# Long-convolution and recurrence block on one core: one position sum per tile, and the filter network issued ahead of the first chunk

## The chip, the core and the metric

The kernel runs on one core of a Trainium2 chip. A core has five engines with queues of their own, which run in order: PE (matmul), DVE (vector), ACT (scalar), POOL (GpSimd) and SP, which here only issues transfers. ACT issues transfers too. The metric is the device time of one execution in microseconds (us); lower is better.

## The reference

4096 tokens of 1024 columns get a position table added (512 columns by grid row, 512 by grid column), are normalised and modulated, and go through one input projection. One half of its columns feeds a long convolution with a filter that a small network makes from the position, the other half a gated recurrence in both directions that starts from the states of 256 context tokens. What matters here:

```python
xl = x + grid_sincos(rows, D)[None]                     # the position sum, 4096 x 1024
pl = (rms_norm(xl, norm_g) * (1.0 + sc_l) + sh_l) @ w_in
pc = (rms_norm(ctx, norm_g) * (1.0 + sc_c) + sh_c) @ w_in
...
h = sin(freq[0] * (z @ f_w1 + f_b1))                    # the filter network, 4096 positions x 64
h = sin(freq[1] * (h @ f_w2 + f_b2))
h = sin(freq[2] * (h @ f_w3 + f_b3))
h = h @ f_w4 * exp(-t * deltas)                         # the filter rows
...
hf_c, hb_c = rglru_bidir(pc[..., r0:r1], *rnn_p, zero, zero)
hf_l, hb_l = rglru_bidir(pl[..., r0:r1], *rnn_p, hf_c[:, -1], hb_c[:, 0])
...
y = concat(rms_norm(long_conv(v * x1, k) * x0) * silu(z_h), rms_norm(hf_l + hb_l) * silu(z_r))
out = rms_norm(xl + g_l * (y @ w_out), final_g)
```

`f_w1` to `f_w3` are 64 columns wide; two halves of the positions share a 128-row tile.

## The kernel before

**Start.** `pass_a` first computes the modulation: `mod` (L319) loads `w_mod` in pieces (tile `wm`, 4 buffers) and multiplies them with the condition, part 1 for the scale `s1`, part 0 for the shift. Beside it the first 512 tokens are loaded as two pairs of tiles (`xload`, L402), and the four blocks of `xr` weights.

**A pair of token tiles.** `xload` loads two tiles of 128 tokens (`xt`, 128x1024) by SP and the row part of the positions (`rp`, L413) by the ACT queue. Its inner function `sums` then adds, on POOL, `rp` to columns 0 to 511 and `self.cpos` to columns 512 to 1023 (L421 and L422; both go through the helper line L463), `squares` takes sums of squares on ACT (L432). `xsplit` (L442) scales on DVE (L454), splits the product into two 16-bit parts (`xh` by ACT, L456; `xlo` by POOL, L458) and transposes both by DMA into the chunk tile `X` (L459, L460). Tokens come to `X` by these transposes alone, and `X` of a chunk must be whole before its first matmul.

**Chunks.** Eight chunks of 512 tokens follow. Each has 12 weight blocks (4 `xr`, then 4 pairs `x1`, `v`); a block is 24 matmuls of 128x512 (`inproj`) and a short convolution on ACT and DVE (`conv`, L529 to L542). One block is one step: `tick` (L571) runs what `at` has put on that step. In chunk 0 the weights are still being prepared (`wprep`, L484, L489), and the context tokens go through the same weights (`ctx_in`, matmuls named `R` and `I`).

**The filter.** `mlp` (L830) is the network as a generator with ten stops: for each half of the positions three layers, each on two tiles of 512 columns, then two stops that split the result and write it to `hD`. One tile of one layer is two f32 matmuls (`fb<-x` or `fa<-x`), ACT's `Identity` (L849), five DVE operations (L850 to L854) and ACT's `Sin` (L855); a result is split by L861, L862 and L864 and written by ACT-issued transfers (L868 to L875). Before, its ten stops are pulled at steps 1 to 10 (`ML`, `MK`). `filt` at step `FS` = 10 sets up the filter's constants (`filter_setup`, loads L881 to L898), and 16 groups of 4 filter rows follow from step `FS + FG`, one group every `FD` = 4.95 steps (`filter_group`, `filter_row`). A row takes 3 f16 matmuls (`fa<-whl,hb`), 2 f32 matmuls (`fb<-kd,st`) and two passes each on ACT and DVE, and POOL adds it to `acc`.

**Order.** Within the bounds of the steps a scheduler sets the order of every engine; each queue then runs in that order on the chip. After the eight chunks the Fourier transforms, the backward recurrence and the output follow, which the change does not touch.

Of the kernel before, what the change touches and what calls it, by code (L numbers as in the profile page):

```python
# [10 lines left out]
F32 = mybir.dt.float32  # L11
# [11 lines left out]
D = 1024  # L23
# [6 lines left out]
CT = 5  # L30
ML = 1
MK = 1
FS = 10
RQ = 1
OD = 7
OP1 = (0, 0)
# [11 lines left out]
MS = ()  # L48
XS = ((1, 1, 2), (1, 2, 3))
PB = {"mm": 3, "fa": 2, "fb": 2, "sm": 1}  # L50
FD = 4.95
XK = ((6, 9), (0, 4))
NX = 11
D0 = (8, 11, 12, 13, 14, 16, 17, 17)
# [109 lines left out]
class K:  # L164
# [237 lines left out]
    def xload(self, pool, src, pos, xts=None, rp=None, lag=None):  # L402


        nc = self.nc
        xts = xts or [pool.tile([128, D], F32, name="xt", bufs=2) for k in range(2)]
        ss = pool.tile([128, 2], F32, name="ss", bufs=2)
        if pos is not None:
            q = nc.scalar if rp is not None or RQ else nc.sync
            rp = pool.tile([128, 2, 512], F32, name="rp", bufs=1) if rp is None else rp  # L410
            t = self.a["t_pos"]
            for h in range(2):
                q.dma_start(rp[64 * h:64 * h + 64], bass.AP(  # L413
                    tensor=t.tensor, offset=t.offset + 512 * (2 * pos + h), ap=[[0, 64], [1024, 2], [1, 512]]))
        for k in range(2):
            xt = xts[k]
            nc.sync.dma_start(xt, src[128 * k:128 * k + 128])

        def sums():
            for k, xt in enumerate(xts):  # L420
                self.padd(xt[:, :512], xt[:, :512], rp[:, k])  # L421
                self.padd(xt[:, 512:], xt[:, 512:], self.cpos)  # L422
                if pos > 3:
                    nc.sync.dma_start(self.xpD[128 * (pos + k):128 * (pos + k) + 128], xt)

        def squares():
            with ExitStack() as es:
                if lag and IA[0]:
                    es.enter_context(self.tc.issue_after(self.eva))
                for k in range(2):  # L430
                    xh = pool.tile([128, D], F16, name="xh", bufs=2)
                    nc.scalar.activation(xh, xts[k], AF.Square, accum_out=ss[:, k:k + 1])  # L432
        if lag:
            self.at(lag[0], sums)
            self.at(lag[1], squares)
        else:
            if pos is not None:
                sums()
            squares()
        return xts, ss  # L440
# [144 lines left out]
    def pass_a(self):  # L585
        tc, nc, a = self.tc, self.nc, self.a
        with ExitStack() as es, ExitStack() as right:
            ap = es.enter_context(tc.tile_pool(name="ap", bufs=1))
# [8 lines left out]
            ml = ml_.__enter__()  # L597
            sp_ = tc.tile_pool(name="start", bufs=1)
            sp = sp_.__enter__()
            if True:  # L600
                self.columns(sp)
                self.tap_sums()
                m = self.mod(sp, ml, ap, 1)
                next(m)
                self.cpos = ap.tile([128, 512], F32, name="cpos")
                for h in range(2):
                    nc.scalar.dma_start(self.cpos[64 * h:64 * h + 64], a["t_pos"])
                xt = [hy.tile([128, 1028], F32, name="xc", bufs=4)[:, :D] for k in range(3)]
                xr = [self.xload(ap, tok(0), 0, xt[:2], xt[2].rearrange("p (k c) -> p k c", k=2)),
                      self.xload(ap, tok(2), 2)]  # L610
                raw = self.xp_.tile([128, NB, 8, 128], F32, name="X", bufs=2)
                for j in range(NB):
                    nc.sync.dma_start(raw[:, j], a["w_in"][COLS["xr"] + j])
                self.pull(m)
                m = self.mod(sp, ml, ap, 0)
                next(m)
                for k in range(2):
                    self.xsplit(ap, xr[k], self.s1, self.sx, dst(X, 2 * k))
                gs = [self.wprep("xr", j, raw[:, j]) for j in range(NB)]
                for k in range(2):  # L620
                    for j, g in enumerate(gs):
                        W["xr", j] = next(g)
                self.pull(m)
                for g in gs:
                    next(g)

            def wpair(k):
                raw = sp.tile([128, 2, 8, 128], F32, name="wm", bufs=4)
# [13 lines left out]
            def filt():  # L642
# [4 lines left out]
                next(g)  # L647
                for d in FL:
                    self.at(d, lambda: next(g))
            mlp = self.mlp(ml)  # L650
            for k in range(4):
                self.at(k, lambda k=k: wpair(NB + 2 * k))
            self.at(3, recur)
# [2 lines left out]
            ctx = self.ctx_in(ap, hy, W)  # L656
            for d in (0, 2, 4):
                self.at(CT + d, lambda: next(ctx))
            for k in range(10):
                self.at(ML + k // MK, lambda: self.pull(mlp, 1))  # L660
            self.at(FS, filt)
            for n in range(16):
                self.at(FS + FG + int(FD * n), lambda n=n: self.filter_group(self.flt, n))
# [163 lines left out]
        return zip(*[self.unit(rn, [(0, 2 * p), (0, 2 * p + 1)], n, xcs[p], fin((2 * p, 2 * p + 1))) for p in range(2)])  # L827


    def mlp(self, pool):  # L830
        nc, a = self.nc, self.a
        ws = pool.tile([128, D], F32, name="bm", bufs=1)[:, :384].rearrange("p (l c) -> p l c", l=3)
        nc.scalar.dma_start(ws, a["f_w"])
        fc = pool.tile([128, 6], F32, name="fc")
        nc.vector.tensor_mul(fc[:, 0:3], self.col[:, 104:107], self.col[:, 107:110])
        nc.vector.tensor_copy(fc[:, 3:6], self.col[:, 107:110])
        for half in range(2):
            H = []
            for c in (2 * half, 2 * half + 1):
                z = pool.tile([66, 512], F32, name="x", bufs=4)  # L840
                nc.scalar.dma_start(z, a["t_z"][:, 512 * c:512 * c + 512])
                H.append(z)
            for l in range(3):
                for c in range(2):
                    ps = self.pst("fa" if c % 2 else "fb", 2)
                    self.mms(ps, ws[:66 if l == 0 else 128, l, :], H[c], True, True)
                    x = pool.tile([128, 512], F32, name="x", bufs=4)
                    q = pool.tile([128, 512], F32, name="q", bufs=3)
                    nc.scalar.activation(x, ps, AF.Identity, bias=fc[:, l:l + 1], scale=fc[:, 3 + l:4 + l])  # L849
                    nc.vector.tensor_scalar(q, x, INV2PI, MAGIC, op0=OP.mult, op1=OP.add)  # L850
                    nc.vector.tensor_scalar(q, q, -MAGIC, None, op0=OP.add)
                    nc.vector.scalar_tensor_tensor(x, q, -C1, x, op0=OP.mult, op1=OP.add)
                    nc.vector.scalar_tensor_tensor(x, q, -C2, x, op0=OP.mult, op1=OP.add)
                    nc.vector.tensor_scalar(x, x, PI_IN, -PI_IN, op0=OP.min, op1=OP.max)  # L854
                    nc.scalar.activation(x, x, AF.Sin)  # L855
                    H[c] = x
                yield
            for c in (2 * half, 2 * half + 1):
                h = H[c % 2]
                hl = pool.tile([128, 2, 512], F16, name="q", bufs=3)  # L860
                nc.scalar.activation(hl[:, 0], h, AF.Copy)  # L861
                nc.vector.tensor_sub(hl[:, 1], h, hl[:, 0])  # L862
                hr = pool.tile([128, 2, 512], F16, name="q", bufs=3)
                nc.vector.tensor_copy(hr, hl[:, :, ::-1])  # L864
                lv = hl.rearrange("p x (n m) -> p x n m", m=64)
                rv = hr.rearrange("p x (n m) -> p x n m", m=64)
                n0 = 8 * c
                nc.scalar.dma_start(self.hD[0:64, :, n0:n0 + 8, :], lv[0:64])  # L868
                nc.scalar.dma_start(self.hD[0:64, :, 32 + n0:40 + n0, :], lv[64:128])
                nc.scalar.dma_start(self.hD[64:128, :, 25 - n0:33 - n0, :], rv[64:128])  # L870
                k = 7 if c == 0 else 8
                nc.scalar.dma_start(self.hD[64:128, :, 57 - n0:57 - n0 + k, :], rv[0:64, :, 0:k, :])
                if c == 0:
                    nc.scalar.dma_start(self.hD[64:128, :, 0, 1:64], rv[0:64, :, 7, 0:63])
                    nc.scalar.dma_start(self.hD[64:128, :, 0, 0:1], rv[0:64, :, 7, 63:64])  # L875
                yield
# [85 lines left out]
    def filter_l1(self, pool, kd):  # L962

        nc = self.nc
        ps = self.pst("sm", 1)
        for b in range(NB):
            self.mm(ps[:, b:b + 1], self.acc[:, 128 * b:128 * b + 128], self.ones[:, 0:1], True, True)
        self.rl = self.cp.tile([128, NB], F32, name="rl")
        nc.vector.tensor_copy(self.rl, ps[:, :NB])
        nc.vector.reciprocal(self.rl, self.rl)  # L970
        ps = self.pst("sm", 1)
        self.mm(ps[0:1, :], self.ones[:, 0:1], self.acc, True, True)
        br = pool.tile([1, 512], F32, name="br", bufs=1)
        nc.scalar.dma_start(br, self.a["hy_bias"])
        nc.vector.tensor_mul(br, ps[0:1, :], br)
        nc.vector.tensor_add(kd[0:1, :], kd[0:1, :], br)
# [544 lines left out]
```

## Time and profile before

| | |
|---|---|
| median of 3 runs | 2239.83 us (2232.47 to 2243.20) |
| the profiled execution, its own time | 2242.97 us |
| its span from the first to the last instruction | 2241.2 us |
| mean granted clock of TensorE over the span | 0.943 of full speed |
| PE, DVE, ACT, POOL busy | 86%, 61%, 52%, 28% of the span |

The profile is of one execution. A span lies 1.8 us inside that execution's time. A row of the timeline says when an instruction started, how long it took, and in brackets how long its engine had been idle before it and what ended that. A row of a group says how often it ran, its busy time and the mean of one; matmul rows overlap a little, so sums of such rows are upper bounds of the engine's busy time. Granted clock 1.00 is 2.4 GHz; below that, part of a stretch ran at 1.2 GHz.

### The profile page before, as it was taken

How to read it: one execution, taken by the hardware profiler on the slowest of the kernel's cores; microseconds unless marked ns; L12 is line 12 of the kernel's file. 1: busy time of each engine (PE TensorE's matmuls, PEld its weight loads, DVE VectorE, ACT ScalarE, POOL GpSimd, SP SyncE). 2: the span in 40 equal slices, each digit the busy share in tenths (PEclk: the TensorE clock that was granted, in tenths of full speed). 3: DMA queues.
4: the chain of work that ended last, by engine and by line, in shares of the span. 5: the costliest groups of instructions: out<-in, count | busy, mean ns of one | idle time of the engine just before them, and what ended most of it. 6: DMA issues, size and time to landing. Idle time of an engine off the chain costs nothing. (4 is left out here: it accounts for less than half of the span.)

```text
span 2241.2 us, 30015 instructions
## 1 busy us (share of the span) xinstructions
PE 1934.0 (86%) x10640; PEld 933.0 (42%) x10640; DVE 1362.1 (61%) x2629; ACT 1173.0 (52%) x1828; POOL 623.2 (28%) x417
## 2 busy tenths in 40 slices
PE   6866989989889899878888989898898858999997
PEld 2443434434334344333334545454443434444443
DVE  3894676756647567564543663744745565766576
ACT  2655766664656578576573733744556531432232
POOL 3024344343424321111211342533423300111130
PEclk9987989999999999989999999999999879999999
DMA  9547354565544522666746889889998798344332
GB/s 286 196 123 209 102 184 136 179 171 150 191 126 129 141 90 84 204 184 196 219 147 212 200 202 253 216 217 232 236 234 229 186 264 234 112 143 150 115 125 104
DMA packets 397028, 398.43 MB, mean 178 GB/s; under 512 B 208809, under 2 KB 295359, under 8 KB 392270
## 3 DMA queue, kind: packets, MB, share of 16 engines
q1 hardware_dynamic: 381020, 356.93, 56.4%
q10 hardware_dynamic: 15858, 39.59, 6.0%
q8 instruction: 84, 1.38, 0.3%
q14 instruction: 66, 0.54, 0.1%
HBM read 206.62 MB, written 146.81 MB: 158 GB/s over the span
## 5 line engine op out<-in xcount | busy, mean ns | idle before, releaser
L169 PE MATMUL mm<-X,wh 128*128 128x512 f16 x3072 | 733.4, 386 | 32.2 <-DVE cvx L536 10.2
L169 PEld LDWEIGHTS <-wh 128*128 128x128 f16 x3648 | 325.8, 100 | 455.5 <-issue 93.4
L169 PE MATMUL mm<-X,wz 128*128 128x512 f16 x1536 | 371.9, 389 | 9.8 <-ACT zh L1023 5.0
L169 PEld LDWEIGHTS <-wz 128*128 128x128 f16 x1728 | 158.2, 100 | 226.7 <-issue 58.8
L169 PEld LDWEIGHTS <-hl 128*128 128x128 f16 x1536 | 149.7, 99 | 222.7 <-issue 37.8
L169 PE MATMUL mm<-wz,hl 128*128 128x512 f16 x768 | 176.7, 385 | 18.4 <-DVE oxt L1445 6.9
L169 PE MATMUL mm<-X,hl 128*128 128x512 f16 x768 | 174.7, 382 | 9.5 <-DMA hl<-hlD 9.5
L463 POOL TENSOR_TENSOR acc<-acc,dec 128x512 f32<-128x512 f32 x64 | 88.1, 1377 | 237.2 <-ACT dec L941 227.7
L463 POOL TENSOR_TENSOR oacc<-oacc,osq 128x512 f32<-128x512 f32 x21 | 38.5, 1833 | 330.9 <-ACT oacc L1417 327.8
L466 POOL TENSOR_TENSOR I<-I,xc 128x1024 f32<-128x1024 f32 (+3 forms) x36 | 84.4, 2348 | 161.4 <-ACT I L788 155.0
L169 PE MATMUL fa<-xc,gw 128*128 128x512 f32 (+3 forms) x152 | 79.2, 614 | 46.2 <-DVE cvv L531 19.4
L1201 POOL TENSOR_TENSOR A<-A,B 128x256 f32<-128x256 f32 x64 | 53.1, 829 | 229.1 <-DVE B L1200 194.9
L458 POOL TENSOR_TENSOR xlo<-xt,xh 128x1024 f16<-128x1024 f32 x32 | 74.3, 2344 | 140.1 <-ACT xh L456 140.1
L169 PE MATMUL fb<-tb,vki 128*128 128x128 f16 x768 | 98.2, 225 | 14.6 <-DMA tb<-in_t_s 9.8
L169 PE MATMUL fa<-tb,vu 128*128 128x128 f16 x768 | 97.7, 225 | 0.0
L812 DVE TENSOR_TENSOR_SCAN I<-R,car,I 128x512 f32<-128x512 f32 (+2 forms) x64 | 97.2, 1540 | 0.1
L1212 DVE SCALAR_TENSOR_TENSOR yy<-A,yy 128x512 f16<-128x512 f32 x64 | 56.6, 885 | 64.6 <-ACT yy L1211 64.5
L1199 DVE TENSOR_TENSOR A<-fa,kf 128x512 f32<-128x512 f32 x64 | 43.9, 686 | 81.0 <-ACT kf L1195 78.1
L169 PEld LDWEIGHTS <-vki 128*128 128x128 f16 x768 | 77.2, 101 | 29.5 <-issue 17.9
L466 POOL TENSOR_TENSOR zr<-zr,sg 128x1024 f32<-128x1024 f32 x16 | 39.5, 2466 | 175.7 <-ACT sg L1069 140.9
L169 PE MATMUL fb<-xc,gw 128*128 128x512 f32 (+3 forms) x152 | 77.8, 601 | 10.2 <-ACT I L788 5.0
L463 POOL TENSOR_TENSOR hf<-hf,I 128x1024 f32<-128x1024 f32 x16 | 50.0, 3127 | 129.1 <-DVE I L812 82.2
(345 smaller groups left out, 3420.8 us busy)
## 6 DMA issues: line engine op xcount, KB each, us to landing
VkD<-vk SPq DMA_DIRECT2D x64, 256.0 KB, 2.4
VuD<-vo SPq DMA_DIRECT2D x64, 256.0 KB, 2.6
X<-XD SPq DMA_DIRECT2D x8, 2048.0 KB, 9.6
vu<-VuD SPq DMA_DIRECT2D x128, 128.0 KB, 3.7
vki<-VkD SPq DMA_DIRECT2D x128, 128.0 KB, 3.3
ZD<-zo SPq DMA_DIRECT2D x64, 256.0 KB, 3.5
xt<-in_x SPq DMA_DIRECT2D x30, 512.0 KB, 5.0
xpD<-xt SPq DMA_DIRECT2D x28, 512.0 KB, 3.7
```

Source lines behind the costliest of these rows:

```text
L169: self.nc.tensor.matmul(out, lhsT, rhs, start=start, stop=stop)
L458: nc.gpsimd.tensor_sub(xl, xt, xh)
L463: self.nc.gpsimd.tensor_add(out, x, y)
L466: self.nc.gpsimd.tensor_mul(out, x, y)
L812: nc.vector.tensor_tensor_scan(f(h), f(r), f(h), 0.0 if c is None else c, op0=OP.mult, op1=OP.add)
L1199: nc.vector.tensor_mul(A, u4, kf[:, :, 0:1, :].to_broadcast([128, NB, 2, 64]))
L1201: nc.gpsimd.tensor_sub(A[:, :, 0, :], A[:, :, 0, :], B[:, :, 1, :])
L1212: nc.vector.scalar_tensor_tensor(yy[:, :, 1, :], yv, 0.125, yy[:, :, 0, :], op0=OP.mult, op1=OP.subtract)
```

## The change

It does three things. For all token pairs but the first, one POOL operation of 1024 columns adds both parts of the positions from a tile `pos` (128x2x1024) that keeps the column part in its right half and takes the row part of each pair into its left. The network `mlp` is started before the modulation of part 1 is pulled and ended before the first chunk's steps; its weights lie in a fourth buffer of `xc`. And the filter's setup moves from step 10 to 5, with a group of rows every 5.2 steps instead of 4.95. The bias row of the filter takes a buffer of `vk`.

```diff
-FS = 10
+FS = 5
-FD = 4.95
+FD = 5.2
@@ xload
-            rp = pool.tile([128, 2, 512], F32, name="rp", bufs=1) if rp is None else rp
+            whole = rp is None
+            rp = self.pos[:, :, :512] if whole else rp
...
             for k, xt in enumerate(xts):
-                self.padd(xt[:, :512], xt[:, :512], rp[:, k])
-                self.padd(xt[:, 512:], xt[:, 512:], self.cpos)
+                if whole:
+                    self.padd(xt, xt, self.pos[:, k])
+                else:
+                    self.padd(xt[:, :512], xt[:, :512], rp[:, k])
+                    self.padd(xt[:, 512:], xt[:, 512:], self.cpos)
@@ pass_a
-                self.cpos = ap.tile([128, 512], F32, name="cpos")
+                self.pos = ap.tile([128, 2, D], F32, name="pos")
                 for h in range(2):
-                    nc.scalar.dma_start(self.cpos[64 * h:64 * h + 64], a["t_pos"])
+                    for k in range(2):
+                        nc.scalar.dma_start(self.pos[64 * h:64 * h + 64, k, 512:], a["t_pos"])
+                self.cpos = self.pos[:, 0, 512:]
...
+                mlp = self.mlp(ml, hy.tile([128, 1028], F32, name="xc", bufs=4)[:, :384].rearrange("p (l c) -> p l c", l=3))
+                self.pull(mlp, 1)
                 self.pull(m)
                 m = self.mod(sp, ml, ap, 0)
                 next(m)
+                self.pull(mlp, 5)
                 for k in range(2):
                     self.xsplit(ap, xr[k], self.s1, self.sx, dst(X, 2 * k))
...
                 for g in gs:
                     next(g)
+                self.pull(mlp)
...
-            mlp = self.mlp(ml)
...
-            for k in range(10):
-                self.at(ML + k // MK, lambda: self.pull(mlp, 1))
@@ mlp
-    def mlp(self, pool):
+    def mlp(self, pool, ws):
-        ws = pool.tile([128, D], F32, name="bm", bufs=1)[:, :384].rearrange("p (l c) -> p l c", l=3)
@@ filter_l1
-        br = pool.tile([1, 512], F32, name="br", bufs=1)
+        br = pool.tile([1, 512], F32, name="vk", bufs=2)
```

The scheduler's order shows what this moves. On DVE, at the first `xsplit`, before (L454 is the scaling, L489 a weight's low part):

```order
L315 SCALAR_TENSOR_TENSOR rq_x<-rt_x,rq_x 128x2 x2
L295 TENSOR_SCALAR sw<-col,es 128x4
L454 SCALAR_TENSOR_TENSOR xc<-xc,rq_x,s_149 128x1024 x2
L454 SCALAR_TENSOR_TENSOR xt<-xt,rq_x,s_149 128x1024 x2
L489 SCALAR_TENSOR_TENSOR wh<-X,p2s_w,wh 128x1024
```

and in the change (L458 is the scaling now, L856 to L860 a network layer's five operations, L868 and L870 the split of a result):

```order
L458 SCALAR_TENSOR_TENSOR xc<-xc,rq_x,s_149 128x1024
L856 TENSOR_SCALAR q<-x 128x512 x2
L857 TENSOR_SCALAR q<-q 128x512 x2
L858 SCALAR_TENSOR_TENSOR x<-q,x 128x512 x2
L859 SCALAR_TENSOR_TENSOR x<-q,x 128x512 x2
L860 TENSOR_SCALAR x<-x 128x512 x2
L458 SCALAR_TENSOR_TENSOR xc<-xc,rq_x,s_149 128x1024
L315 SCALAR_TENSOR_TENSOR rq_x<-rt_x,rq_x 128x2 x2
L358 TENSOR_TENSOR mr<-mm,bm 2x256
L458 SCALAR_TENSOR_TENSOR xt<-xt,rq_x,s_149 128x1024
L868 TENSOR_TENSOR q<-x,q 128x512
L458 SCALAR_TENSOR_TENSOR xt<-xt,rq_x,s_149 128x1024
```

The third layer stands between the first and the second scaling; the first two layers stand ahead of both. In all, nine of the network's twelve layer tiles stand ahead of the first chunk's first matmul on PE, and three behind it.

On ACT, the copies `xh` of the same four tiles, before (L456):

```order
L456 ACTIVATE xh<-xc 128x1024
L484 ACTIVATE wh<-X,p2s_w 128x1024
L456 ACTIVATE xh<-xc 128x1024
L413 DMA rp<-in_t_pos 64x2x512
L456 ACTIVATE xh<-xt 128x1024 x2
```

and in the change (L460; L855, L861, L867 are the network's):

```order
L460 ACTIVATE xh<-xc 128x1024
L460 ACTIVATE xh<-xt 128x1024
L874 DMA hD<-q 128x1x512
L875 DMA hD<-q 128x1x512
L876 DMA hD<-q 128x1x512
L878 DMA hD<-q 128x1x448
L880 DMA hD<-q 128x1x63
L881 DMA hD<-q 128x1x1
L867 ACTIVATE q<-x 128x512
L460 ACTIVATE xh<-xt 128x1024
```

The last of the four copies now stands behind six transfers of the network's result.

On ACT, late in chunk 0, before (L881 to L898 are the filter's loads, L788 the context's gates):

```order
L542 ACTIVATE hax_1976<-cvx_1970,sg_1193 128x2
L881 DMA st_1991<-in_t_s1f 128x128
L883 DMA dl<-in_t_delta 128x512
L885 DMA dcol<-in_t_dec 128x64
L897 DMA dec<-in_t_delta 128x512
L898 DMA dec<-in_hy_bias 128x512
L788 ACT_TABLE_LOAD
```

In the change these loads stand some 40 rows ahead of the gates' table load, among the convolutions of the fifth to eighth block, and four of the 64 filter rows stand ahead of chunk 1.

## Rows read from the trace of the kernel before

**Rows 1.** Stages: us; busy PE, PEld, DVE, ACT, POOL; PE clock, DMA share, GB/s.

```profile
0.00:62.00 62.00, 38.54 (x148) 13.86 (x149) 26.93 (x93) 20.56 (x30) 20.62 (x16) 0.89 1.00 281
62.00:135.00 73.00, 69.47 (x555) 33.60 (x555) 63.93 (x224) 43.45 (x72) 0.11 (x1) 0.98 0.49 163
135.00:208.50 73.50, 43.04 (x284) 29.48 (x284) 45.35 (x98) 36.40 (x70) 32.87 (x20) 0.81 0.61 153
208.50:805.90 597.40, 537.69 (x2174) 235.18 (x2175) 388.47 (x684) 383.02 (x647) 235.59 (x143) 0.95 0.50 151
```

**Rows 2.** PE's waits, 62 to 208.5 us: total, times, longest.

```profile
PE mm L169 <- DVE xc L536: 7.1, 1, 7.1
PE fa L169 <- ACT R L788: 6.5, 1, 6.5
PE fb L169 <- ACT x L855: 4.4, 2, 2.3
PE mm L169 <- DMA R<-xlo: 3.4, 1, 3.4
PE fa L169 <- ACT x L855: 2.4, 2, 1.4
```

**Rows 3.** PE's timeline: the first matmuls of chunks 0 and 1.

```profile
61.98 4.01 PE L169 MATMUL mm<-X,wh 128*128 128x512 f16 x11 [0.34 <-DMA X<-xh]
...
208.56 1.46 PE L169 MATMUL mm<-X,wh 128*128 128x512 f16 x3 [8.90 <-DMA X<-xh]
```

**Rows 4.** DVE's five operations of the network: count, duration ns min/median/max.

```profile
L850 DVE TENSOR_SCALAR q<-x x12: 410/418/427, 85.5 to 157.8; 128x512 f32<-128x512 f32 x12
L851 DVE TENSOR_SCALAR q<-q x12: 412/418/429, 86.0 to 158.7; 128x512 f32<-128x512 f32 x12
L852 DVE SCALAR_TENSOR_TENSOR x<-q,x x12: 677/682/1750, 86.5 to 159.7; 128x512 f32<-128x512 f32 x12
L853 DVE SCALAR_TENSOR_TENSOR x<-q,x x12: 681/683/2487, 88.8 to 160.6; 128x512 f32<-128x512 f32 x12
L854 DVE TENSOR_SCALAR x<-x x12: 414/418/1680, 91.3 to 161.4; 128x512 f32<-128x512 f32 x12
```

**Rows 5.** The load stretch: timelines of DVE and ACT.

```profile
36.79 0.15 DVE L180 TENSOR_SCALAR p2h_sx<-s1q 128x1 int32<-128x1 int32 x1 [4.61 <-ACT gr L395]
...
53.41 1.06 ACT L456 ACTIVATE xh<-xt 128x1024 f16<-128x1024 f32 x1 [9.10 <-DMA X<-xh]
```

**Rows 6.** ACT's and PE's groups of the network, and the issue of a result's transfer.

```profile
L855 ACT ACTIVATE x<-x 128x512 f32<-128x512 f32 x12 | 7.5, 625 | 9.4 <-DVE x L854 9.3
L849 ACT ACTIVATE x<-fb,fc 128x512 f32<-128x512 f32 x6 | 4.6, 773 | 3.9 <-PE fb L169 3.8
L169 PE MATMUL fa<-x,bm 128*128 128x512 f32 (+1 forms) x12 | 7.5, 712 | 2.4 <-ACT x L855 2.4
L169 PE MATMUL fb<-x,bm 128*128 128x512 f32 (+1 forms) x12 | 7.3, 693 | 4.4 <-ACT x L855 4.4
...
L869 ACTq DMA_DIRECT2D hD<-q x4: 587/616/622, 119.9 to 176.3; - x4
```

**Rows 7.** PE's groups of the filter rows, 208 to 880 us, all 64 rows.

```profile
L169 PE MATMUL fb<-kd,st 128*128 128x512 f32 x128 | 65.6, 594 | 0.4 <-DVE vk L955 0.4
L169 PE MATMUL fa<-whl,hb 128*128 128x512 f16 x192 | 59.7, 379 | 0.0
```

**Rows 8.** ACT at the end of chunk 0: behind the filter's loads.

```profile
187.82 1.28 ACT L788 ACT_TABLE_LOAD   x1 [3.96 <-DMA dec<-in_f_w]
```

**Rows 9.** POOL's groups by shape, whole span, and one row of its timeline.

```profile
L466 POOL TENSOR_TENSOR I<-I,xc 128x1024 f32<-128x1024 f32 x28 | 68.5, 2448 | 123.0 <-ACT I L788 116.6 <-DVE rq_x L315 6.3
L463 POOL TENSOR_TENSOR xt<-xt,cpos 128x512 f32<-128x512 f32 x30 | 44.1, 1469 | 5.2 <-DMA xt<-in_x 5.2
L463 POOL TENSOR_TENSOR xt<-xt,rp 128x512 f32<-128x512 f32 x30 | 41.5, 1383 | 82.8 <-DMA xt<-in_x 57.2 <-issue 24.2 <-DMA rp<-in_t_pos 1.4
...
134.89 6.42 POOL L458 TENSOR_TENSOR xlo<-xt,xh 128x1024 f16<-128x1024 f32 x2 [76.14 <-ACT xh L456]
```

## The prediction

> **What bounds the kernel now.** I read the stages first, then PE's waits in the stage that the change touches, then the timelines around them. The stages [rows 1] tell where there is something to gain. Until 62 us the core loads: the DMA engines are busy all the time, PE 38.54 us and DVE 26.93 us of 62. From 62 to 135 us PE is busy 69.47 us of 73 and DVE 63.93. From 135 to 208.5 us PE is busy only 43.04 us of 73.5, at a mean clock of 0.81. In chunks 1 to 6 (208.5 to 805.9 us) PE is busy 537.69 us of 597.4, 90%: PE bounds them, and DVE has slack (65%). So what the change can win lies between the first matmul of chunk 0, at 61.98 us, and that of chunk 1, at 208.56 us [rows 3]: 146.6 us, of which PE works 112.5 (69.47 + 43.04) and waits 34.1. The waits are for the network itself (4.4 + 2.4 us, for ACT's `Sin`), for a convolution of the context on DVE (7.1), for the context's gates on ACT (6.5), for a transposed context tile (3.4) [rows 2], and 8.90 us for chunk 1's tile [rows 3]; the rest is 1.4.
>
> The network's DVE work lies in that same stretch. One layer tile takes 0.418 + 0.418 + 0.682 + 0.683 + 0.418 = 2.62 us by the medians [rows 4], twelve of them 31.4 us, all between 85 and 162 us.
>
> **The change part by part.** The profiled execution took 2242.97 us, which is 3.1 above the median of the three runs; the sum is made against 2243.
>
> *The start of chunk 0.* By the order, three layers on two tiles stand on DVE ahead of the last scalings of the first 512 tokens, and six transfers on ACT ahead of the last copy. In series that is 6 x 2.62 = 15.7 us on DVE; per layer one `Identity` and one `Sin` that nothing of the other tile hides, 3 x (0.773 + 0.625) = 4.2; per layer one tile on PE, (7.5 + 7.3) / 12 = 1.23, so 3.7; and 6 x 0.616 = 3.7 us of issuing [rows 6]. Together 27.3 us. Against it stands slack: DVE sat idle 4.61 us before the scale was ready, and ACT 9.10 us before the third copy, because a transpose was late [rows 5]. This leaves 27.3 - 13.7 = 13.6; I take 13, and chunk 0 starts at 75 us. The ends are 0 (DVE has 35 us free in this stretch [rows 1], were all of it usable) and 27.3 (no slack usable).
>
> *From there to chunk 1.* PE's work: nine of twelve layer tiles have gone ahead, -9 x 1.23 = -11.1. Four filter rows come in; a row is 65.6/64 + 59.7/64 = 1.96 us [rows 7], so +7.8. With half of the waits gone I expect 135 to 208 us to run at the 0.95 of chunks 1 to 6 in place of 0.81 [rows 1]: 43.04 x (1 - 0.81/0.95) = 6.3 less (the ends are 0 and this). 112.5 - 11.1 + 7.8 - 6.3 = 102.9. Waits: the network's 6.8 go. Of the 6.5 for the gates, 3.96 was ACT held by the filter's loads [rows 8], which now stand far ahead of the gates, so 2.5 stay. Of the 7.1 and the 3.4 I let 2 stay each, because DVE has three quarters of the network less to do ahead of them; both ends, none and all, are kept. The 8.90 and the 1.4 stay: chunk 1's tile still needs two pairs of token tiles after each other, each with a load, sums, squares, scaling and copies. 2.5 + 2 + 2 + 8.9 + 1.4 = 16.8. So 102.9 + 16.8 = 119.7, chunk 1 starts at 75 + 119.7 = 194.7 in place of 208.6: **-14 us**.
>
> *Chunks 1 to 7.* They hold 60 filter rows in place of 64: 4 x 1.96 = 7.8 us of PE, of which I count the 90% in which PE bounds: **-7 us** (the ends are 0, if the rows lie where PE waits, and -8).
>
> *One sum per tile.* For 30 tiles two POOL operations of 1.469 and 1.383 us become one. Of the same kind and size there is a product of two f32 tiles, 128x1024 in 2.448 us [rows 9]. That is 0.4 us less per tile, 12 us of POOL's busy time. I cost it at nothing: POOL is busy 235.59 of 597.4 us in the chunks [rows 1], so it has time to spare. If each pair's sums ended the wait for a chunk's tile, 4 tiles x 0.4 = 1.6 us per chunk would be won, 11 us over seven chunks; that is the lower end. The cost that could stand against it is a longer hold-up of DVE: beside POOL's two operations of 3.2 us at 134.89 us [rows 9], one of DVE's 0.683 us operations took 2.487 [rows 4]. A hold of 2.448 in place of 1.469 us could add up to 0.98 us to a DVE operation, once per tile.
>
> The Trainium skill ("SBUF — State Buffer", "SBUF: two separate sides") says that DVE and GpSimd share one port pair as an exclusive lock that is held for a whole instruction, and that the loser blocks fully. By that rule the merged sum speaks against itself on DVE, and the time would be that of the rival on the lock below; the stretched operation agrees with it.
>
> *The rest at nothing.* Two more position transfers of 128 KB and the network's weights, 192 KB, move into the load stretch: 0.45 MB at its 281 GB/s [rows 1] is 1.6 us, inside the bounds of the start. The bias row in a buffer of `vk` makes one small load wait for a store, once, at the end of chunk 7, under ACT's other work.
>
> Sum: -14 - 7 = -21, so 2243 - 21 = **2222 us**. Against the median that is -18, or 0.8%.
>
> **The rivals.** A measurement of this kernel can tell about 0.5%, 11 us, from no change.
>
> *No change.* The waits are those of the context's chain (load, sums, scaling, transposes, one pair after the other) and not of DVE's load; then only the network's 6.8 go and the clock stays: 75 + 109.2 + 27.3 = 211.5, +3, with the rows -7: 2239 us. For it: on DVE the context's operations need each other's results and would leave gaps in any case. Against it: DVE is busy 88% of 62 to 135 us, and the network stands among those operations. That part of the network does not move (three layer tiles of twelve stay behind the first matmul) belongs here.
>
> *Slower: the load stretch has no slack to give.* PE, ACT and DVE each run in order, so each layer holds up what stands behind it: modulation matmuls on PE, copies on ACT, scalings on DVE. If none of the 13.7 us can be used, chunk 0 starts at 62 + 27.3 = 89.3; with the waits of the rival above chunk 1 starts at 89.3 + 109.2 + 27.3 = 225.8, +17; with the rows -7 that is +10: 2253 us. It decides from where the start's delay exceeds what the stretch behind wins, 146.6 - 136.5 + 7 = 17 us, so from a first matmul later than 79 us. For it: the network's layers and the scalings interleave on DVE in the order. Against it: the 9.10 us in which ACT waited for transposes, and the transposes for loads that are then done.
>
> *Faster.* The start moves by only 5 us, since a DVE that is half idle takes the layers up beside the loads, and of the waits only the 8.90 stays: 67 + 102.9 + 8.9 = 178.8, -30, rows -8: 2205 us. For it: the idle time. Against it: the layers are a chain over three engines.
>
> *The longer hold.* If the 0.98 us falls on what PE waits for in every one of the 28 tiles that are summed beside chunks, 27 us are added to the forecast: 2249 us. For it: PE's last waits are often for DVE. Against it: DVE has 35% slack in the chunks, and two short holds block about as often as one long one.
>
> **How the numbers follow.** Chances: the forecast 0.45, no change 0.22, faster 0.13, slower by the start 0.12, the longer hold 0.08. Faster by over 0.5% is the faster case, most of the forecast (0.41) and a little of the no-change case (0.04): 0.58. Slower by over 0.5% is the start (0.12) and half of the hold with an edge of the others: 0.17. 0.25 remains. The range takes the forecast with its bounds (the start's 0 and 27.3 alone are -13 and +14 around it), the faster case at its low end and the no-change case and the hold at its upper end: 2204 to 2250, and leaves out the slower case and an edge beyond the faster one.
>
> **What would show it.** The first matmul of chunk 0 near 75 us (right if 70 to 79), that of chunk 1 near 195; no wait of PE for `Sin` after chunk 0 has run for 30 us; the table load of the context's gates without 4 us of idle time; a clock above 0.9 between the two; POOL's sums as one operation of about 2.4 us; four rows' less PE work from chunk 1 on, and all that follows chunk 7 earlier by the same amount. The forecast is wrong if chunk 0 starts later than 79 us, or if chunk 1 starts later than 203 us although chunk 0 started as said: then the context's chain, not DVE, was the bound.

## The result, and the profile after

The changed kernel takes 2210.58 us (median of 6 runs, 2207.72 to 2216.44); the kernel before, 2235.43 us beside it (6 runs). The ratio is 0.9891, 95% interval 0.9866 to 0.9916: faster by 1.1%, about 25 us. The prediction was 2222 us and "faster", range 2204 to 2250.

The time lies in the range, but the stages do not lie where the prediction put them. I cut both profiled executions into four stretches at three marks: the first matmul of chunk 0, that of chunk 1, and the first matmul that reads the filter's spectrum (`tb`, `vki`) after the eight chunks and the forward transforms. From that last mark on, PE's order is the same, instruction by instruction, in every kernel of this document. The view is the one of stretches; its columns are start:end, length, then busy us (and instructions) of PE, PE's weight loads, DVE, ACT and POOL, granted clock, DMA share, GB/s. The kernel before, cut at its own marks:

```profile
0.00:61.98 61.98, 38.52 (x147) 13.84 (x148) 26.91 (x93) 20.54 (x30) 20.62 (x16) 0.89 1.00 281
61.98:208.56 146.58, 112.53 (x839) 63.11 (x840) 109.30 (x321) 79.93 (x141) 32.98 (x20) 0.90 0.55 158
208.56:1231.70 1023.14, 909.36 (x4016) 402.36 (x4016) 626.36 (x1129) 647.15 (x1015) 316.21 (x180) 0.95 0.53 160
1231.70:2241.20 1009.50, 873.55 (x5640) 453.74 (x5638) 599.55 (x1087) 425.38 (x644) 253.35 (x201) 0.94 0.71 192
```

The changed kernel:

```profile
0.00:80.17 80.17, 51.13 (x168) 17.75 (x168) 47.48 (x141) 30.45 (x46) 23.86 (x14) 0.83 0.93 281
80.17:208.17 128.00, 108.15 (x844) 61.26 (x845) 96.00 (x287) 75.31 (x137) 37.07 (x20) 0.92 0.52 151
208.17:1206.69 998.52, 895.32 (x3992) 399.40 (x3993) 618.96 (x1116) 637.05 (x1000) 299.25 (x152) 0.96 0.53 163
1206.69:2205.80 999.11, 869.81 (x5640) 450.93 (x5638) 599.23 (x1087) 425.66 (x644) 254.45 (x201) 0.95 0.72 194
```

| stretch | before | after | difference | predicted |
|---|---|---|---|---|
| start to chunk 0 | 61.98 | 80.17 | +18.2 | +13 |
| chunk 0 to chunk 1 | 146.58 | 128.00 | -18.6 | -26.9 |
| chunk 1 to the mark `vki` | 1023.14 | 998.52 | -24.6 | -7 |
| rest, order unchanged | 1009.5 | 999.1 | -10.4 | 0 |

So nothing is won by chunk 1 (208.56 against 208.17 us), and the gain comes behind it: of the 24.6 us, 21.2 lie ahead of the first matmul of the forward transforms (`fa<-ut,st1u`, at 933.7 and 912.1 us). I count the last line as scatter: over the 14 profiled kernels this last stretch takes 999 to 1010 us, though the order of PE, ACT and POOL in it is the same. One doubt stays. The three kernels with two sums a tile are the longest there (1009.5 to 1010.1 us; the others 999.0 to 1004.2, and one 1007.7). Their profiled executions also lay 2.6 to 7.5 us above the medians of their kernels, and that of the 1007.7 lay 6.6 above, so this need not be the sum's doing; it is not excluded. Up to the mark the difference is 25.0 us, as much as between the medians (24.9). Below I therefore read parts from the first three stretches and the whole from the medians.

The start, in the timeline of ACT (start, us, instruction, in brackets the idle time before it and what ended that):

```profile
63.38 0.57 ACTq L874 DMA_DIRECT2D hD<-q  x1
...
69.23 0.62 ACTq L881 DMA_DIRECT2D hD<-q  x1
69.89 0.63 ACT L867 ACTIVATE q<-x 128x512 f16<-128x512 f32 x1 [6.00 <-DMA hD<-q]
70.43 1.04 ACT L460 ACTIVATE xh<-xt 128x1024 f16<-128x1024 f32 x1
```

and of PE:

```profile
77.06 2.08 PE L169 MATMUL fb<-x,xc 128*128 128x512 f32 x2 [8.56 <-ACT x L861]
80.17 2.07 PE L169 MATMUL mm<-X,wh 128*128 128x512 f16 x4 [1.04 <-DMA X<-xh]
...
208.17 0.81 PE L169 MATMUL mm<-X,wh 128*128 128x512 f16 x3 [3.97 <-issue]
```

The last copy of the first 512 tokens (70.43) stands on ACT behind six transfers of the network, during which ACT does no other work for 6.00 us. Its transposes follow, and chunk 0 starts when the last has landed.

PE's waits from there to 212 us (engine, what it waited for, us in total, times, longest) answer to [rows 2]:

```profile
PE mm L169 <- DVE xc L540: 8.6, 3, 7.6
PE mm L169 <- issue: 4.0, 1, 4.0
PE fa L169 <- ACT whl L917: 2.9, 1, 2.9
PE fa L169 <- ACT R L795: 1.5, 1, 1.5
PE mm L169 <- DMA X<-xh: 1.0, 1, 1.0
```

The network's waits are gone and that for the gates is down from 6.5 to 1.5 us; that for the context's convolution has grown from 7.1 to 8.6; that for chunk 1's tile fell from 8.90 [rows 3] to 3.97. In the last, "issue" is the name for a wait whose end the profile does not show.

### The profile page after: what moved, and what is told of

Same layout as the page of the kernel before. It is cut to its first block, busy times and chain, and to the rows that moved or that the text cites. A ratio compares the mean times of both kernels' runs of the same rounds, so it can differ in the third digit from the quotient of the medians.

```text
span 2205.8 us, 29950 instructions
## 1 busy us (share of the span) xinstructions
PE 1924.4 (87%) x10640; PEld 929.3 (42%) x10640; DVE 1361.7 (62%) x2629; ACT 1168.5 (53%) x1825; POOL 614.6 (28%) x387
## 5 line engine op out<-in xcount | busy, mean ns | idle before, releaser
L169 PE MATMUL mm<-wz,hl 128*128 128x512 f16 x768 | 177.3, 386 | 18.2 <-DVE oxt L1451 6.6
L467 POOL TENSOR_TENSOR xt<-xt,pos 128x1024 f32<-128x1024 f32 x30 | 73.3, 2462 | 82.5 <-DMA xt<-in_x 58.6
## 6 DMA issues: line engine op xcount, KB each, us to landing
vu<-VuD SPq DMA_DIRECT2D x128, 128.0 KB
vki<-VkD SPq DMA_DIRECT2D x128, 128.0 KB
```

The lines of the kernel that those rows point to most:

```text
L169: self.nc.tensor.matmul(out, lhsT, rhs, start=start, stop=stop)
L467: self.nc.gpsimd.tensor_add(out, x, y)
```

## The experiments

The change has three parts: the network early (N), the filter's rows earlier and sparser (F), and one sum per tile (S). The title names N and S only. The theories of the first four runs: A, F gives the gain; B, S gives it; D, the longer hold of S costs something; and the prediction's own, N. In what follows "stretch" is chunk 0 to chunk 1, and "chunks" is chunk 1 to the mark `vki`: chunks 1 to 7 and the forward transforms.

### Two sums a tile again (N and F)

```diff
-                if whole:
+                if False:
```

> The changed kernel with two POOL sums of 512 columns a tile again; network and filter rows as changed. Theory A (the earlier and sparser filter rows give the gain; the sum is hidden, as the prediction costed it): 2211 us, within 5. Theory B (the shorter work on POOL gives it: ACT, which the trace shows held for a tile's sum in pass A, is let go sooner): 2231 us, and chunks 1 to 6 take 584 us again in place of 563. Chunk 0's first matmul stays at 80 us by both. Theory D (the long hold on DVE costs something): below 2211.

Measured: 2218.6 us, ratio to before 0.9918 (0.9888 to 0.9948). Between A and B: F carries most of the gain. POOL's groups (count, busy us, mean ns, idle before), first of this kernel, then of the changed one:

```profile
L467 POOL TENSOR_TENSOR xt<-xt,pos 128x512 f32<-128x512 f32 x60 | 82.4, 1400 | 82.5 <-DMA xt<-in_x 54.0 <-issue 23.7 <-DMA VkD<-vk 4.9
```

```profile
L467 POOL TENSOR_TENSOR xt<-xt,pos 128x1024 f32<-128x1024 f32 x30 | 73.3, 2462 | 82.5 <-DMA xt<-in_x 58.6 <-issue 14.1 <-DMA VkD<-vk 5.0
```

A merged sum takes 2462 ns in place of 2 x 1400. D falls: two sums are not faster, and DVE's busy time in the chunks is 622.46 us here and 618.96 in the changed kernel, so the longer operation does not stretch DVE's work.

### The filter at its old steps (N and S)

```diff
-FS = 5
+FS = 10
-FD = 5.2
+FD = 4.95
```

> The changed kernel with the filter at its old steps (setup at 10, a group every 4.95 steps); network early and one sum per tile as changed. Theory A: 2233 us, chunks 1 to 6 at 580 us or more. Theory B: 2213 us, chunks 1 to 6 near 565 us. By both the first matmul of chunk 1 comes some 7 us earlier than the changed kernel's 208 us, because four filter rows of 1.96 us leave chunk 0.

Measured: 2225.99 us, 0.9963 (0.9945 to 0.9980). Between the theories again: without F 15 us are lost. Chunk 1 does not start 7 us earlier, as both theories had it, but at 210.26; from chunk 0's start the stretch is only 2.5 us shorter (125.5 against 128.0). PE's row says why:

```profile
210.26 4.97 PE L169 MATMUL mm<-X,wh 128*128 128x512 f16 x14 [10.20 <-DMA X<-xh]
```

Without filter rows PE waits 10.20 us for chunk 1's tile, with four rows 3.97. They fill a wait. The mark flatters this a little: without the rows, 3.9 us of gate matmuls of 511 columns stand ahead of chunk 1's first matmul, and with them behind it.

### One sum a tile alone (S)

```diff
-                self.padd(xt[:, :512], xt[:, :512], rp[:, k])
-                self.padd(xt[:, 512:], xt[:, 512:], self.cpos)
+                if whole:
+                    self.padd(xt, xt, self.pos[:, k])
...
-        br = pool.tile([1, 512], F32, name="br", bufs=1)
+        br = pool.tile([1, 512], F32, name="vk", bufs=2)
```

> The kernel before with one sum of 1024 columns a tile alone (and the buffer of the bias row that makes room for it). Theory A: 2235 us, as before. Theory B: 2213 us, chunks 1 to 6 near 565 us, first matmul of chunk 0 at 62 us as before. Theory D: above 2240.

Measured: 2230.72 us, 0.9972 (0.9954 to 0.9990): a small gain of 5 us, far from B, on the other side of D.

### The network early alone (N)

The two edits of the first two experiments together.

> The kernel before with the network early alone. The prediction's own account (the network's removal from chunk 0 gives most of the gain): 2215 to 2221 us. Theories A and B alike: 2235 us within 5, since the traces show the start 18 us later and the stretch to chunk 1 18.6 us shorter; chunk 0's first matmul near 80 us, chunk 1's at 201 to 209 us.

Measured: 2232.33 us, 0.9978 (0.9960 to 0.9995). The prediction's own account falls: the network's move by itself is worth 4 us, as A and B had it. Its stretches:

```profile
0.00:80.82 80.82, 50.86 (x167) 17.83 (x168) 47.50 (x141) 30.40 (x46) 24.41 (x16) 0.82 0.96 278
80.82:205.81 124.99, 104.62 (x831) 57.27 (x832) 90.82 (x283) 80.90 (x149) 31.10 (x20) 0.91 0.51 149
205.81:1223.13 1017.32, 903.93 (x4003) 400.55 (x4004) 624.49 (x1120) 642.08 (x995) 318.31 (x180) 0.96 0.53 161
```

Start +18.8, stretch -21.6 against the kernel before.

The three parts, from the medians: N 4 us (alone), S 5 to 8 (alone 5.4, on N 6.3, on N and F 8.0), F 14 to 15 (on N 13.7, on N and S 15.4). Differences of a few us between two of these kernels are inside the intervals. N, S on N and F on both add up to the whole because each is measured from the one before; F does not have one worth of its own, since without N it brings only 8 us (S alone against S and F, below).

### F in two: earlier, or sparser

Two runs keep N and S and take one half of F each.

```diff
-FD = 5.2
+FD = 4.95
```

> The changed kernel with a group of filter rows every 4.95 steps again, setup at step 5: after the first two groups every group stands on the step on which another group stood before, only one group more lies in chunk 0 and none at the end of chunk 7. Theory A1 (the gain of the earlier filter is the number of rows that PE has to take in the bound chunks, about 3.7 us for each of four): 2211 us, within 5. Theory A2 (the gain is where the rows stand against the token sums, i.e. the sparser spacing: ACT is held less in front of the decay tiles): 2224 to 2228 us, like the kernel with the old steps.

```diff
-FS = 5
+FS = 10
```

> The changed kernel with the setup at step 10 as before, but a group every 5.2 steps: no row in chunk 0, the last group in chunk 7 at step 90 in place of 86. Theory A1: 2224 to 2228 us, as with the old steps, since 64 rows stand in chunks 1 to 7 again. Theory A2: 2211 to 2216 us.

Measured: earlier but dense 2218.98 us, 0.9928 (0.9900 to 0.9956); sparse but late 2220.65 us, 0.9940 (0.9922 to 0.9959). Each is between the two theories: both halves count. The chunks of four kernels, old steps first, then earlier and dense:

```profile
210.26:1224.53 1014.27, 906.96 (x4003) 402.37 (x4004) 617.99 (x1119) 640.80 (x993) 303.94 (x156) 0.95 0.53 161
```

```profile
208.93:1215.16 1006.23, 899.74 (x3991) 399.80 (x3992) 608.94 (x1117) 635.10 (x999) 298.59 (x152) 0.95 0.53 162
```

late and sparse:

```profile
205.62:1214.25 1008.63, 908.08 (x4004) 403.00 (x4004) 622.83 (x1119) 641.47 (x993) 304.98 (x156) 0.95 0.53 162
```

and the changed kernel 998.52, PE 895.32 (above). Four rows out of the chunks take 7.2 us from PE's busy time (906.96 to 899.74) and leave its idle time (length less busy) at 107.3 and 106.5; stretch and chunks together are 6.7 us shorter. Sparser rows leave PE's work and take from its idle time: 107.3 to 100.6. So one half of F is work moved, the other, where it stands alone, waits avoided.

### S and F, the network left in chunk 0

```diff
-ML = 1
-MK = 1
-FS = 10
+ML = 0
+MK = 2
+FS = 5
...
-FD = 4.95
+FD = 5.2
```

This is the one-sum kernel with these steps.

> The kernel before with the sum of 1024 columns and the filter at the change's steps, the network left in chunk 0 and pulled twice a step so that it ends by step 5. If the network's early place is worth nothing by itself (2232 against 2236 with it alone): 2212 to 2218 us, first matmul of chunk 0 near 62 us, of chunk 1 near 210. If the early filter needs the network out of chunk 0 (its rows must wait there for the network's writes): 2222 us or more, with a first matmul of chunk 1 later than 215 us.

Measured: 2222.35 us, 0.9949 (0.9932 to 0.9965), at the border between the two cases; the first matmul of chunk 1 comes at 219.24, so the numbers of the second one hold.

```profile
64.69:219.24 154.55, 122.85 (x866) 64.71 (x866) 115.53 (x334) 91.29 (x158) 35.84 (x20) 0.89 0.56 156
219.24:1216.99 997.75, 896.60 (x3991) 399.27 (x3992) 621.88 (x1117) 636.03 (x999) 298.65 (x152) 0.96 0.53 163
```

The chunks are as short as in the changed kernel (997.75 against 998.52). But with the network in chunk 0 the stretch is 8.3 us longer with the rows than without (146.23 with one sum alone), with the network gone by 2.5. The first of these two differences also holds the network's faster pull. The reason given, that the rows wait for the network's writes, is not what the waits show: PE is busy 122.85 us in the stretch against 111.75 with one sum alone, and idle 31.7 against 34.5. The rows' work came on top and filled next to nothing. By the medians the network's early place is worth 4 us alone and 12 together with S and F.

### Seven rows in chunk 0

```diff
-FS = 5
+FS = 3
-FL = (2, 3)
+FL = (1, 2)
-FG = 2
+FG = 1
...
-                self.at(FS + FG + int(FD * n), lambda n=n: self.filter_group(self.flt, n))
+                self.at(FS + FG + (4 * n if n < 2 else 11 + int(5.4 * (n - 2))), lambda n=n: self.filter_group(self.flt, n))
```

> The changed kernel with the setup at step 3 and groups at steps 4 and 8, then one every 5.4 steps from 15: 7 rows in chunk 0 in place of 4. Theory A1: 3 rows at 3.7 us less in the bound chunks, chunk 0 longer by 1 to 6 us: 2200 to 2207 us. Theory A2: within 5 of 2211 us, in either direction. If chunk 0 has no room for more rows: 2211 to 2217 us, with its stretch longer by 6 us or more.

Measured: 2209.28 us, 0.9888 (0.9866 to 0.9910): the same time as the changed kernel. A2's time holds, A1 falls. The stretches say why:

```profile
78.98:213.87 134.89, 114.75 (x862) 63.82 (x862) 100.21 (x295) 83.69 (x154) 41.52 (x24) 0.93 0.53 150
213.87:1201.05 987.18, 898.32 (x3973) 398.36 (x3974) 613.40 (x1109) 629.41 (x985) 296.42 (x148) 0.95 0.53 164
```

The chunks win 11.3 us, chunk 0 loses 6.9. In chunk 0 PE's busy time grows by 6.6 us and its idle time stays (19.85 and 20.14). By PE's matmuls the growth is that of two rows (24 `fa<-whl,hb` and 12 `fb<-kd,st` in place of 18 and 8: 3.6 us) and of the 511-column gate matmuls (4.1 us), which are back ahead of chunk 1. The wait for chunk 1's tile, which took up the first rows, is 3.52 us and does not shrink further. So the new work filled no wait there. The 11.3 us of the chunks are all PE's idle time (103.2 to 88.9; busy it is 3.0 us longer, with fewer matmuls). How much of that is the spacing of 5.4 steps, and how much the rows gone, this run does not separate.

### Who holds ACT

In the changed kernel ACT stands still three times for 8.4 to 8.8 us in chunks 2 to 4, each time ahead of a filter row's absolute value:

```profile
368.16 0.63 ACT L947 ACTIVATE dec<-kd 128x512 f32<-128x512 f32 x1 [8.82 <-POOL xt L467]
461.23 0.63 ACT L947 ACTIVATE dec<-kd 128x512 f32<-128x512 f32 x1 [8.54 <-POOL xt L467]
555.10 0.63 ACT L947 ACTIVATE dec<-kd 128x512 f32<-128x512 f32 x1 [8.40 <-POOL xt L467]
```

In the kernel before, such a hold ends with the issue of a pair's row positions, which stands on ACT's queue until POOL has summed the pair that uses the tile now:

```profile
561.58 0.60 ACTq L413 DMA_DIRECT2D rp<-in_t_pos  x1
562.23 0.63 ACT L941 ACTIVATE dec<-kd 128x512 f32<-128x512 f32 x1 [9.58 <-POOL xt L463]
```

My theory (H) was that S and the sparser rows both work by shortening this hold. Three runs move the issue off ACT: to SP, to POOL, and to POOL with dense rows.

```diff
-RQ = 1
+RQ = 0
```

> The changed kernel with the pairs' row positions loaded by SP's queue in place of ACT's. Theory H (what both the sum and the spacing work on is one hold: the issue of the next pair's positions stands on ACT's queue until POOL's sums of this pair are done, 8.4 to 8.8 us three times in chunks 2 to 4, and the convolutions behind it make PE wait): the holds go from ACT, PE's idle time from chunk 1 to the forward transform falls from 57 us by 10 to 25, and the time to 2188 to 2202 us, unless SP, held in its turn, delays the token loads. Rival P (ACT would wait there in any case, since its next work needs POOL's additions that stand behind the sums): within 5 of 2211 us.

```diff
-            q = nc.scalar if rp is not None or RQ else nc.sync
+            q = nc.scalar if rp is not None else nc.gpsimd
```

> The changed kernel with the row positions issued by POOL's own queue, where they stand right behind the sums that free their tile and so hold nothing up. Theory H: ACT's waits of 8 us ahead of a row's absolute values go, and the time is 2188 to 2202 us. Rival P: within 5 of 2211 us.

> As the one with the positions on POOL's queue, but with a group of rows every 4.95 steps again. With the positions on ACT the dense spacing cost 8 us (2219 against 2211). Theory H: without the hold the spacing is worth nothing, so within 4 of the kernel with the positions on POOL and 5.2 steps. Rival P (the spacing works on something else, such as DVE's or ACT's load by itself): 7 to 10 us above it.

Measured: 2213.22 us, 0.9891 (0.9865 to 0.9917) from SP; 2217.02 us, 0.9916 (0.9895 to 0.9937) from POOL; 2224.9 us, 0.9956 (0.9938 to 0.9975) from POOL and dense. H falls. The holds did go: with the issue on POOL, ACT's waits for POOL's token sums from 206 to 914 us are

```profile
ACT xh L436 <- POOL xt L467: 17.1, 9, 3.3
```

3.3 us at most, ahead of the squares; those of a group's decay tiles for the filter's additions on POOL (`dec` for `acc`) grew from 21.6 us in the changed kernel to 27.7. With the issue on SP the holds are gone too, and these waits are 31.9 us. The chunks do not notice:

```profile
212.46:1208.67 996.21, 893.00 (x3991) 399.00 (x3992) 622.86 (x1117) 639.56 (x1002) 316.07 (x174) 0.96 0.54 164
```

996.21 against 998.52 us, PE's idle time 103.2 in both. By the medians the spacing is still worth its 8 us (2224.9 against 2217.0), as P had it; by the chunks of the two profiles it is worth 4 (1000.3 against 996.2), where it was 7.7 with the issue on ACT. So H is out as the source of the gain, while a part of the hold in the spacing's worth is not excluded. By P's times the kernel with SP's issue is inside, that with POOL's is 1 us outside. The long hold was real, and taking it away won nothing.

### The first tokens ahead of the network

```diff
-                self.pull(mlp, 5)
                 for k in range(2):
                     self.xsplit(ap, xr[k], self.s1, self.sx, dst(X, 2 * k))
+                self.pull(mlp, 5)
```

> The changed kernel with the scaling and transposing of the first 512 tokens written ahead of the network's five stops, so that the start does not wait for them; the network's rest then runs beside the first blocks. In the changed kernel chunk 0 starts at 80 to 86 us and chunk 1 at 208 to 212. Theory C (the network is work that the first 210 us must hold, wherever it stands): the start comes 8 to 15 us earlier, the stretch to chunk 1 is as much longer, and the time stays within 5 of 2211 us. Theory L (the late start is a loss of its own, and chunk 0 has room for the rest of the network): start near 70 us, chunk 1 at 198 to 203 us, 2200 to 2205 us.

Measured: 2217.76 us, 0.9937 (0.9913 to 0.9961; the kernel before took 2231.06 beside it). L falls, and C was too mild: chunk 0 starts 6 us earlier, at 74.0, and lasts 14 us longer.

```profile
74.00:215.95 141.95, 115.51 (x859) 64.77 (x857) 104.92 (x319) 80.14 (x143) 35.38 (x20) 0.89 0.54 156
215.95:1214.75 998.80, 898.90 (x3992) 400.55 (x3992) 620.06 (x1117) 636.84 (x1000) 298.69 (x152) 0.95 0.53 163
```

Ahead of chunk 0 PE has little to do (51.13 us of 80.17 in the changed kernel); inside it the network's rest stands among the context's work: PE is busy 7.4 us more, and its waits for the context's transposed tiles are 9.0 us in place of 0.5. So the late start of the changed kernel is not a loss to be mended in this way. No run is clearly faster than the changed kernel.

## Why the prediction was right in its time and wrong in its reasons

**The start (+13 forecast, +18.2 measured).** The series of 27.3 us was a fair upper bound; the step that failed is the slack of 13.7 us, of which 9 were usable here, and 3 to 10 in the other profiles with the network at this place (starts of 79.0 to 85.9 us). The six transfers of a half cost ACT 6.00 us, where I counted 3.7 of issuing. They stand ahead of the fourth copy, while the slack of 9.10 us had been ahead of the third [rows 5]. The start passed the 79 us from which the rival "slower" was to decide, and the kernel was faster all the same: that rival's point rested on a gain of 7 us in the chunks.

**From chunk 0 to chunk 1 (-26.9 forecast, -18.6 measured).** The network's PE time was right: 14.53 us of its matmuls stand behind the first matmul of chunk 0 before, 3.15 after, so -11.4 for -11.1. The network's 6.8 us of waits went and the gates' wait fell below the 2.5 I left it. Three terms were wrong.

Of the clock's 6.3 us, 2.7 came, at the gates. From 135 us to chunk 1 the granted clock rose from 0.81 [rows 1] to 0.91, near the 0.95 I put there. Most matmuls took the same time in both (the 96 of `mm<-X,wz` 379 ns each). Those of the gates did not; the rows are a group and a stretch, first before, then after:

```profile
L169 PE MATMUL fa<-xc,gw 128*128 128x256 f32 x16 | 6.4, 491 | 6.5 <-ACT R L788 6.5
189.65:194.80 5.15, 5.15 (x12) 4.17 (x13) 0.00 (x0) 3.40 (x8) 2.04 (x2) 0.51 0.26 50
```

```profile
L169 PE MATMUL fa<-xc,gw 128*128 128x256 f32 x16 | 4.9, 386 | 1.5 <-ACT R L795 1.5
192.40:197.80 5.40, 5.40 (x25) 4.55 (x25) 5.06 (x11) 5.40 (x16) 3.59 (x3) 1.00 0.13 51
```

Before, PE ran these matmuls for 5.15 us at a granted clock of 0.51 after waiting 6.51 us; in the change it waited 1.48 us and they ran at 1.00, so the 32 took 9.7 us in place of 12.4. Behind the wait for the context's convolution nothing changed: 24 `mm<-R,wh` took 2.72 us before and 2.74 after, at 0.52 and 0.50, against 1.50 us for 24 of them 13 to 18 us earlier in either kernel. My mean over the stage charged the low clock to all of the 43.04 us; it stood in the waits and in the matmuls right behind them, and one of the two long waits stayed.

That wait, for the context's convolution, was 8.6 us where I left 2. It did shrink with the network gone, against the rival "no change": with the network in chunk 0 and no rows it is 7.1 us, and 11.3 with one sum alone; with the network gone and no rows (three kernels) 3.4 to 5.9; with the network gone and the rows there (four kernels with the positions on ACT's queue) 6.5 to 9.1. One sum alone, then N and S:

```profile
PE mm L169 <- DVE xc L540: 11.3, 1, 11.3
```

```profile
PE mm L169 <- DVE xc L540: 3.4, 3, 2.4
```

So the step was right for the network, and it left out the rows that come into the same stretch. By what path they bring the wait back is not shown.

And "the 8.90 stays" was wrong on the good side: of the four rows, put at +7.8, some 6 us went into that wait (10.20 to 3.97), and the stretch grew by 1.2 to 2.5.

**The network as the source of the gain.** By the sum, N was to bring 17.7 us (+13 at the start, -30.7 behind it) and F 3.2 (+7.8 for the rows, -7 in the chunks, -4.0 for the filter's loads ahead of the gates). The runs show 4 for N alone and 14 to 15 for F on it. N is worth more only where it makes room for F's rows: 12 us with S and F in place. My no-change rival, less the rows, puts chunk 1 at 203.7 us; N alone has it at 205.81.

**Four rows less (-7 forecast).** Right: PE's busy time in the chunks falls by 7.2 us by the earlier start of the rows alone, and the chunks by 8.0. What I did not price at all is the other number of F in the diff, the spacing of 5.2 steps: 4 to 8 us of the chunks (6 late, 8 early, 4 with the positions on POOL), late, all of it out of PE's idle time; in the early pairs about half shows as busy time of PE at the same count of matmuls. I saw rows only as work; where they stand counts too, and which waits the spacing shortens is not shown.

**One sum, costed at nothing, lower end -11.** Measured 5 to 8 us by the medians. "POOL has time to spare" is true of the stage, and it was the wrong question. PE's idle time in the chunks falls by 9.7 us with S alone, by 6.1 on N, by 2.3 on N and F. On N and F the chunks are only 2.0 us shorter where the medians differ by 8.0, so where the rest lies is open. The rival of the longer hold is out. By the sums' rows POOL is busy 9 us less, and the first sum of a pair still waits for its load; which of PE's waits the shorter sum ends is not shown. With S in place, taking the hold off ACT's queue won nothing; the two-sum kernels were not tried without it.

**In sum.** -14 by chunk 1 became 0, and -7 behind it became -25. The two errors stood against each other, and that the time came out inside the range is luck: of the 11 us by which the forecast of 2222 was off, the stages make only 4, and the rest is that the sum started from an execution of 2243 where the median of six is 2235.43. Its own test had said it: "wrong if chunk 0 starts later than 79 us". Others of its signs came: no wait for `Sin` in chunk 0, the gates' table load without idle time, a clock of 0.92 between the two marks, sums of 2.46 us. Chunk 1 near 195 us did not (208.17). What stays open is the path by which the spacing, and S, shorten PE's waits.

## What to carry to other kernels

Ask of every moved piece of work not only where it goes but which wait it will fill there: the first four rows filled some 6 of the 10 us for which PE waited for chunk 1's tile, and the work put there after them filled nothing and came on top. Price the small numbers of a schedule (here a spacing) as changes of their own, and test the parts singly, and in pairs, before you believe a sum that comes out right. A long wait in the trace is a suspect, not a price: three holds of 8.5 us were taken from ACT and PE's idle time stayed at 103.2 us.

## What the runs showed of the hardware

*One operation of 1024 columns costs less than two of 512.* POOL's f32 additions take 2462 ns against 2 x 1400; for the 30 tiles POOL is busy 73.3 us in place of 82.4.

*POOL and DVE hold each other up.* In the start of the changed kernel POOL's 128x1024 subtraction takes 5.17 us beside the network's operations on DVE, and 2.12 us twelve us later without them; a DVE scaling that begins beside the first takes 3.15 us, the next one 1.26:

```profile
54.90 5.17 POOL L462 TENSOR_TENSOR xlo<-xc,xh 128x1024 f16<-128x1024 f32 x1 [19.78 <-ACT xh L460]
...
66.83 2.12 POOL L462 TENSOR_TENSOR xlo<-xt,xh 128x1024 f16<-128x1024 f32 x1
```

```profile
58.00 3.15 DVE L458 SCALAR_TENSOR_TENSOR xc<-xc,rq_x,s 128x1024 f32<-128x1024 f32 x1
...
61.49 1.26 DVE L458 SCALAR_TENSOR_TENSOR xt<-xt,rq_x,s 128x1024 f32<-128x1024 f32 x1
```

The Trainium skill ("SBUF — State Buffer", "SBUF: two separate sides") gives as the cause an exclusive lock on a port pair that both share, which a DVE operation with two inputs in SBUF needs; these rows agree with it. That a longer hold must cost DVE more does not follow: with 30 holds of 2.46 us in place of 60 of 1.40, DVE's busy time in the chunks is 3.5 us lower.

*The same steps give the same chunks.* Five profiled kernels with these rows and one sum (the changed kernel, the positions on SP and on POOL, the network in chunk 0, the first tokens ahead) take 996.2 to 998.8 us from chunk 1 to the mark, while the stretch behind it, in which PE's order is the same, scatters by 9 us over the same five. A part of a few us is read better from such a stretch than from the whole.
